# Gathering the experts' tokens unit by unit in fp32, with 17 instead of 14 weight slots, in a hybrid SSD, attention and expert layer

## The chip, the cores and the metric

The kernel runs on one core of a Trainium2 chip. The metric is the device time of one execution in microseconds, the median of several runs. One execution was also recorded by the hardware profiler; its rows are the ones shown below.

## What is computed

One layer for 512 tokens of width 1024: a norm, a wide projection, a state-space branch and a sliding-window attention branch, both gated and merged, an output projection added to x, a second norm, and 64 experts of which each token uses two. The part that the change touches, shortened:

```python
x = x + merged @ w_out
h2 = rms_norm(x, norm2_g).reshape(b * s, d)     # x * rsqrt(mean(x^2) + eps) * norm2_g
...
xs = h2[tok].reshape(n_blocks, MOE_BLOCK, -1)   # rows gathered by expert
def expert_block(args):
    xb, e = args
    hid = jax.nn.silu(xb @ w_gate_e[e]) * (xb @ w_up_e[e])
    return hid @ w_down_e[e]
...
return x + y_moe
```

## The kernel before, in words

The first 700 us (projections, both branches) are not touched. Then three stages follow.

The output projection (lines 711 to 773) runs over four column tiles `ct` of 256 columns. Its matmuls (L741 to L743) give the new x, which L746 adds to the old x in `acc`, four tiles of 128 tokens by 1024 columns. The same loop transposes x for the router (L751, L754, L758). It also multiplies x by norm2's weights along the row (L767, from `g2t`), and splits the product into a rounded high part (L772, ScalarE) and the rest (L773, GpSimd), both kept in `hx`, two tiles of 16 KB per partition. Each token's own norm factor is a scalar and is applied later, from `rst`, `rr` and `gts`.

The router (L796 to L845) chooses two experts for each token on VectorE and computes `dest`, a place for each of the 1024 assignments: expert e has places from 512 e on, and its first 32 are served by the main loop.

The main loop goes over `units`: 16 units of four experts and, after eight of them, unit 16, which serves 128 more tokens of one expert that has over 32. For each unit
- `group(g)`, called every second unit, gathers the tokens of two units: an indicator matrix `oh` (L879, L880 on VectorE) with 256 columns, and a matmul of `hx`, high and low, with `oh` into PSUM (L888), evicted to `st` (L893). The result is already transposed: 128 rows of the width by 256 slots;
- `products(u)` multiplies by the gate and up weights (L908, four experts side by side in the columns of the array; L903 in unit 16), applies tanh and two VectorE steps (L913 to L915), transposes (L918, L920), multiplies by the down weights (L929; L926 in unit 16) and splits the result for the way back (L934, L935);
- `combine` scatters the rows back with an indicator `wk` (L997, L998): two matmuls into PSUM (L1007, L1008) and an addition into `acc` (L1009) for each of 8 pieces.

The weights come from memory as 195 loads of 1024 KB, 12 for a unit (four experts times two gate/up halves and one down matrix) and 3 for unit 16. They go through a ring of slots: NA = 4 slots "ra", which lie where an early stage had its tiles and can be filled while the output projection still runs, and NB = 10 slots "rb", most of which lie where the output projection has its operands. `load_to` issues the next load (L783, on SyncE's queue) into a slot as soon as its last reader is done; SyncE works its queue in order.

The order of the instructions on each engine is set at build time by a list scheduler: an instruction that is ready in its own forecast of the run may be put ahead of earlier ones that are not. The buffers of a tag (such as the two PSUM buffers "tp", which `group` and `combine` share) go round in the order of the program. In memory the four tiles of `acc`, `hx` and the slots "ra" stand on one side; `oh`, `st`, `wk` and the slots "rb" on the other.

Of the kernel before, what the change touches and what calls it, by code (L numbers as in the profile page):

```python
# [7 lines left out]
F = mybir.dt.float32  # L8
R = mybir.dt.float32r
# [3 lines left out]
AF = mybir.ActivationFunctionType  # L13
# [8 lines left out]
CAP, BLK, NE, NBK, STEP = 32, 128, 64, 32, 512  # L22
POOL_LO, SSD_AHEAD, NA, NB, XGT, UX = 5, 1, 4, 10, 2, 8
PAD = 800
# [6 lines left out]
@with_exitstack  # L31
def tile_hybrid(ctx: ExitStack, tc: tile.TileContext, x, pos, cols, rows, g2d, wrd, wdtd, wcm, wqkv, wso, wao, wo,
                wgu, wdn, out):
    nc = tc.nc
# [50 lines left out]
    G.iota(av, pattern=[[1, 2], [256, 4]], base=1, channel_multiplier=2, allow_small_or_imprecise_dtypes=True)  # L85
    io4 = cp.tile([128, 256], F, name="io4")
    G.iota(io4, pattern=[[STEP, 8], [1, 32]], base=0, channel_multiplier=0, allow_small_or_imprecise_dtypes=True)
    io1 = cp.tile([128, 128], F, name="io1")
# [24 lines left out]
    bx = cp.tile([128, 1], F, name="bx")  # L113
    ixx = cp.tile([128, 3], I32, name="ixx")
    dram = ctx.enter_context(tc.tile_pool(name="dram", bufs=1, space=bass.MemoryType.DRAM))
    h2d = dram.tile([512, 1024], F, name="h2d")
# [583 lines left out]
    ring = [wslot(pr, "ra", NA) for i in range(NA)]  # L700
    hx = [pr.tile([128, 4, 1024], R, name=f"hx{i}") for i in range(2)]
    wrt = [v_(n=288), v_(n=288)]
    g2t = [v_(), v_()]
    for u in range(2):
        S.dma_start(wrt[u], wrd[:, u * 288:(u + 1) * 288])
        S.dma_start(g2t[u], _rows(g2d[u * 512:(u + 1) * 512], 512))
        for k in range(4):
            G.tensor_scalar(wrt[u][:, k * 72:(k + 1) * 72], wrt[u][:, k * 72:(k + 1) * 72],
                            n2g[:, 4 * u + k:4 * u + k + 1], None, op0=OP.mult)
    acc = [pr.tile([128, 1024], F, name=f"acc{t}") for t in range(4)]  # L710
    x2 = [[acc[t][:, u * 512:(u + 1) * 512] for u in range(2)] for t in range(4)]
    for t in range(4):
        nc.sync.dma_start(acc[t], x[t * 128:(t + 1) * 128])
    sx = v_(n=24)
# [9 lines left out]
    for ct in range(4):  # L724
# [4 lines left out]
        cu, cc = ct // 2, slice((ct % 2) * 256, (ct % 2 + 1) * 256)  # L729
        xg, xT = [c_(), c_()], [v_(), v_()]  # L730
        pt = [ptile("tp"), ptile("tp")]
# [30 lines left out]
        elif ct < 3:  # L762
            V.tensor_tensor(lg, lg, pl[:, 0:288], op=OP.add)
        for t in range(4):
            if ct == 3 and t == XGT:
                row_factors()
            (G if ct == 3 else V).tensor_tensor(xg[t // 2][:, (t % 2) * 256:(t % 2 + 1) * 256], x2[t][cu][:, cc],  # L767
                                                g2t[cu][:, cc], op=OP.mult)
        for tp in range(2):
            x3 = xg[tp].rearrange("p (t d) -> p t d", t=2)  # L770
            hi, lo = [hx[i][:, 2 * tp:2 * tp + 2, ct * 256:(ct + 1) * 256] for i in range(2)]
            S.activation(hi, x3, AF.Copy)  # L772
            G.tensor_tensor(lo, x3, hi.bitcast(F), op=OP.subtract)  # L773

# [96 lines left out]

    def group(g):
        dg = dest
        if g:
            dg = pm.tile([128, 8], F, name="dg", tag="dg", bufs=1)
            V.tensor_scalar(dg, dest, -8.0 * STEP * g, None, op0=OP.add)
        oh = pm.tile([128, 4, 256], R, name="oh", tag="oh", bufs=1)
        for t in range(4):
            V.tensor_scalar(oh[:, t], io4, dg[:, t:t + 1], None, op0=OP.is_equal)  # L879
            V.scalar_tensor_tensor(oh[:, t], io4, dg[:, 4 + t:5 + t], oh[:, t].bitcast(F), op0=OP.is_equal, op1=OP.add)  # L880
        st_ = pm.tile([128, 2048], F, name="st", tag="st", bufs=2)
        sts[g] = st_.rearrange("p (k c) -> p k c", k=8)
        for k in range(0, 8, 2):
            p = ptile("y" if g == 0 and k % 4 else "tp")
            for u in range(2):
                for h in range(2):
                    for t in range(4):
                        T.matmul(p[:, u * 256:(u + 1) * 256], hx[h][:, t, (k + u) * 128:(k + u + 1) * 128], oh[:, t],  # L888
                                 start=(h == 0 and t == 0), stop=(h == 1 and t == 3))
            if g == 0 and k % 4:  # L890
                V.tensor_copy(st_[:, k * 256:(k + 2) * 256], p)
            else:
                S.activation(st_[:, k * 256:(k + 2) * 256], p, AF.Copy)  # L893
            yield

    def products(u):
        pg = ptile("mm")
        ga = group(0) if u == 0 else None
        for k in range(8):
            if ga and k % 2 == 0:  # L900
                next(ga)
            if u == 16:
                T.matmul(pg, sts[16][:, k], wt[u, k // 4, 0][:, (k % 4) * 512:(k % 4 + 1) * 512],  # L903
                         start=(k == 0), stop=(k == 7))
                continue
            for e in range(4):
                c = u % 2 * 128 + e * 32
                T.matmul(pg[e * 32:(e + 1) * 32], sts[u // 2][:, k, c:c + 32],  # L908
                         wt[u, k // 4, e][:, (k % 4) * 512:(k % 4 + 1) * 512], start=(k == 0), stop=(k == 7))
# [139 lines left out]
    def over():  # L1049

        dg = pm.tile([128, 8], F, name="dg", tag="dg", bufs=1)
        V.tensor_scalar(dg, dest, bx, None, op0=OP.subtract)
        oh = pm.tile([128, 4, 128], R, name="oh", tag="oh", bufs=1, padded_shape=[128, 4, 256])
        ok = [m_().rearrange("p (t c) -> p t c", t=4) for k in range(2)]
        p = ptile("sb")
        for k in range(2):
            V.tensor_tensor(ok[k], io1[:, None, :].to_broadcast([128, 4, 128]),
                            dg[:, 4 * k:4 * k + 4, None].to_broadcast([128, 4, 128]), op=OP.is_equal)
            for t in range(4):
                T.matmul(p[:, 0:2], ok[k][:, t], rr[:, k, t], start=(k == 0 and t == 0), stop=(k == 1 and t == 3))  # L1060
        V.tensor_copy(rst[:, :, 16], p[:, 0:2])
        V.tensor_tensor(oh, ok[0], ok[1], op=OP.add)
        st_ = pm.tile([128, 1024], F, name="st", tag="st", bufs=2, padded_shape=[128, 2048])
        sts[16] = st_.rearrange("p (k c) -> p k c", k=8)
        for c in range(2):
            p = ptile("tp")
            for k in range(4):
                for h in range(2):
                    for t in range(4):
                        T.matmul(p[:, k * 128:(k + 1) * 128], hx[h][:, t, (4 * c + k) * 128:(4 * c + k + 1) * 128],  # L1070
                                 oh[:, t], start=(h == 0 and t == 0), stop=(h == 1 and t == 3))
            S.activation(st_[:, c * 512:(c + 1) * 512], p, AF.Copy)

    used = 0
    for u in units:
        load_to(used + NA + NB)
        used += 3 if u == 16 else 12
        wk = onehot(u) if u else None
        if u == 16:
            over()  # L1080
        yhl = products(u)
        if u == 0:
            places()
            wk = onehot(0)
        if u == 2:
            count()
        if u % 2 == 0 and u < 14:
            for _ in group(u // 2 + 1):
                pass
        combine(wk, yhl, u)  # L1090

    def extra(i):
# [69 lines left out]
        for t in range(4):  # L1162
            for u in range(2):
                hs = slice(u * 512, (u + 1) * 512)
                ht = m_()
                V.tensor_tensor(ht, hx[0][:, t, hs].bitcast(F), hx[1][:, t, hs].bitcast(F), op=OP.add)
                V.tensor_scalar(ht, ht, rr[:, 0, t, 0:1], 2.0, op0=OP.mult, op1=OP.mult)
                nc.sync.dma_start(h2d[t * 128:(t + 1) * 128, hs], ht)
# [14 lines left out]
        for tl, src, c, n in ((xg, h2d, 4, 512), (o, out, 4, 512), (gt, gwd, 3, 1024)):  # L1183
            V.memset(tl, 0.0)
            G.indirect_dma_start(out=tl, out_offset=None, in_=src, in_offset=at(c), bounds_check=n - 1,
                                 oob_is_err=False)
        xt = pm.tile([128, 1024], F, name="xt", tag="st", bufs=2, padded_shape=[128, 2048])
        for u in range(2):
            p = ptile("tp")
            for k in range(4):  # L1190
                s = slice(k * 128, (k + 1) * 128)
                T.transpose(p[:, s], xg[:, u * 512 + k * 128:u * 512 + (k + 1) * 128], ident)
            V.tensor_copy(xt[:, u * 512:(u + 1) * 512], p)
        p = ptile("mm")
# [27 lines left out]
def _layout(inp):  # L1222
# [14 lines left out]
    def tm(m):  # L1237
# [23 lines left out]
        ("rows", c(rows)),  # L1261
        ("g2", c(f["norm2_g"][0])),
        ("wr", c(wr.reshape(8, 128, 72).transpose(1, 0, 2).reshape(128, 576))),
# [27 lines left out]
```

## Time and profile before

| | before |
|---|---|
| time, median of 3 runs | 1267.71 us (1267.61 to 1268.23) |
| the profiled execution | 1267.16 us, span of its core 1265.4 us |
| TensorE matmul / weight load busy | 93% / 62% of the span |
| VectorE / ScalarE / GpSimd busy | 51% / 31% / 19% |
| read from memory | 266.47 MB, mean 216 GB/s over the span |

Busy shares are averages over stages with different limits: the first 700 us move few bytes, the expert stage moves most of them. The matmuls are recorded with ends that are modelled, so two records may overlap; the spacing of records in the chain is the better price of one.

### The profile page before, as it was taken

To read this page: it belongs to the slowest core of one execution; us is meant where nothing else is said; L and a number is where in the kernel's file an instruction comes from. 1 tells how busy PE (TensorE), PEld (TensorE's weight loads), DVE (VectorE), ACT (ScalarE), POOL (GpSimd) and SP (SyncE) were. 2 spreads that over 40 slices of the span, in tenths; PEclk is the share of its full clock that TensorE was granted. 3 is DMA by queue.
4 is the path that set the end of the run, shared out by engine and by line. 5 is a ranking of instruction groups with operands and counts; after the bars stand their busy time and mean duration, and the time that the engine had idled before them with its cause. 6 is when DMAs were issued, how large, how long until landed. Compare 5 with 4: busy or idle time off the path is not lost.

```text
span 1265.4 us, 16578 instructions
## 1 busy us (share of the span) xinstructions
PE 1177.4 (93%) x6552; PEld 789.3 (62%) x6552; DVE 651.2 (51%) x1224; ACT 388.6 (31%) x796; POOL 237.8 (19%) x189
## 2 busy tenths in 40 slices
PE   6999999999999999999999996989899799989885
PEld 5877878877888878887777994442424244424321
DVE  5956565568526667766647446443342234232422
ACT  5455453454326444534423330210111011101100
POOL 2033431143024522240020131010001000000000
PEclk9999999999999999999999997999999999999998
DMA  4321213211220222212145717999999999999995
GB/s 167 105 89 38 97 67 117 100 67 57 76 101 34 100 68 84 76 64 78 43 167 188 294 55 296 420 415 420 420 419 419 419 416 388 385 414 418 419 419 235
DMA packets 43120, 273.86 MB, mean 216 GB/s; under 512 B 5024, under 2 KB 5664, under 8 KB 11808
## 3 DMA queue, kind: packets, MB, share of 16 engines
q1 hardware_dynamic: 39744, 263.34, 52.7%
q0 software_dynamic: 1712, 7.34, 1.5%
q10 hardware_dynamic: 1584, 2.10, 0.6%
q8 instruction: 52, 0.85, 0.3%
q14 instruction: 28, 0.23, 0.1%
HBM read 266.47 MB, written 6.29 MB: 216 GB/s over the span
## 4 chain that ended last, share of the span: by engine, by line
PE 52%; DMA 6%; DVE 5%; ACT 1%; issue 1%; DVEq 0%; SPq 0%
PE mm L908 10%; PE y L929 6%; PE tp L888 5%; PE mm L197 4%; PE mm L198 4%; PE mm L199 4%; DMA rb<-in_wdn_dram 4%; PE tp L1007 3%; DVE acc L1009 2%; PE tp L1008 2%; PE sb L574 2%; DMA ra<-in_wdn_dram 2%; PE y L620 1%; PE sb L573 1%; PE mm L483 1%; PE mm L485 1%
## 5 line engine op out<-in xcount | busy, mean ns | idle before, releaser
L197 PE MATMUL mm<-h,g 128*128 128x512 f32 x448 | 180.7, 403 | 1.3 <-DVE c L309 1.0
L199 PE MATMUL mm<-h,g 128*128 128x512 f32 x448 | 178.3, 398 | 0.8 <-POOL g L183 0.7
L198 PE MATMUL mm<-h,g 128*128 128x512 f32 x448 | 178.2, 398 | 0.0
L908 PE MATMUL mm<-rb,st 128*32 128x512 f32 x712 | 144.7, 625 | 9.8 <-DMA rb<-in_wgu_dram 9.8
L182 ACT ACTIVATE g<-w 128x1024 fp32r<-128x1024 f32 x100 | 105.6, 1057 | 157.0 <-PE mm L198 113.1
L183 DVE TENSOR_TENSOR g<-w,g 128x1024 fp32r<-128x1024 f32 x78 | 96.8, 1240 | 70.4 <-ACT g L182 66.4
L1009 DVE TENSOR_TENSOR acc<-acc,tp 128x512 f32<-128x512 f32 x132 | 85.9, 684 | 34.4 <-PE tp L1008 34.3
L997 POOL TENSOR_SCALAR wk<-dr,vcol 128x512 fp32r<-128x512 int16 x17 | 26.6, 1565 | 385.4 <-PE tp L1008 347.9
L197 PEld LDWEIGHTS mm<-h,g 128*128 128x128 f32 x448 | 84.4, 188 | 22.7 <-issue 3.8
L199 PEld LDWEIGHTS mm<-h,g 128*128 128x128 f32 x448 | 84.2, 188 | 21.5 <-issue 2.3
L198 PEld LDWEIGHTS mm<-h,g 128*128 128x128 f32 x448 | 84.4, 188 | 18.8 <-issue 2.8
L183 POOL TENSOR_TENSOR g<-w,g 128x1024 fp32r<-128x1024 f32 x22 | 53.8, 2447 | 174.9 <-ACT g L182 143.6
L929 PE MATMUL y<-rb,n 128*32 128x512 f32 x384 | 77.0, 673 | 5.2 <-ACT n L920 3.3
L908 PEld LDWEIGHTS mm<-rb,st 128*32 128x32 f32 x712 | 31.3, 114 | 73.6 <-issue 55.0
L888 PEld LDWEIGHTS tp<-oh,hx 128*128 128x128 f32 x480 | 61.3, 194 | 22.3 <-issue 14.9
L935 DVE TENSOR_TENSOR yo<-y,yo 128x512 fp32r<-128x512 f32 x34 | 23.5, 691 | 99.0 <-ACT yo L934 99.0
L908 PE MATMUL mm<-ra,st 128*32 128x512 f32 x312 | 73.1, 596 | 0.0
L1007 PE MATMUL tp<-yo,wk 128*128 128x512 f32 x132 | 59.2, 465 | 12.7 <-DVE acc L1009 12.5
L888 PE MATMUL tp<-oh,hx 128*128 128x256 f32 x480 | 67.4, 293 | 3.6 <-DVE m L960 3.6
L1007 PEld LDWEIGHTS tp<-yo,wk 128*128 128x128 f32 x132 | 23.6, 187 | 68.9 <-DVE acc L1009 39.5
L913 ACT ACTIVATE n<-mm,rst 128x256 f32<-128x256 f32 x17 | 8.0, 473 | 177.0 <-PE mm L908 169.4
L484 PE MATMUL mm<-g,h 128*128 128x256 f32 x192 | 55.1, 287 | 0.9 <-DVE g L183 0.8
(375 smaller groups left out, 2257.5 us busy)
## 6 DMA issues: line engine op xcount, KB each, us to landing
rb<-in_wgu_dram SPq DMA_DIRECT2D x89, 1024.0 KB, 14.0
rb<-in_wdn_dram SPq DMA_DIRECT2D x48, 1024.0 KB, 16.9
ra<-in_wgu_dram SPq DMA_DIRECT2D x39, 1024.0 KB, 12.2
w<-in_wcm_dram SPq DMA_DIRECT2D x27, 1024.0 KB, 4.9
ra<-in_wdn_dram SPq DMA_DIRECT2D x16, 1024.0 KB, 16.6
w<-in_wso_dram SPq DMA_DIRECT2D x8, 1024.0 KB, 4.9
w<-in_wqkv_dram SPq DMA_DIRECT2D x6, 1024.0 KB, 4.9
gtd<-c POOLq DMA_DIRECT2D x16, 256.0 KB, 2.5
```

The lines of the kernel that those rows point to most:

```text
L182: S.activation(hi[:, :n], src, AF.Copy)
L183: (G if nsp[0] < 3 or nsp[0] % POOL_LO == 0 else V).tensor_tensor(lo[:, :n], src, hi[:, :n].bitcast(F), op=OP.subtract)
L197: T.matmul(p, hi[:, s], mh[k], start=(k == 0), stop=False)
L198: T.matmul(p, hi[:, s], ml[k], start=False, stop=False)
L199: T.matmul(p, lo[:, s], mh[k], start=False, stop=(k == 7))
L484: T.matmul(o, hh[k][:, ts], lo[:, s], start=False, stop=False)
L888: T.matmul(p[:, u * 256:(u + 1) * 256], hx[h][:, t, (k + u) * 128:(k + u + 1) * 128], oh[:, t], start=(h == 0 and t == 0), stop=(h == 1 an ...
L908: T.matmul(pg[e * 32:(e + 1) * 32], sts[u // 2][:, k, c:c + 32], wt[u, k // 4, e][:, (k % 4) * 512:(k % 4 + 1) * 512], start=(k == 0), sto ...
L929: T.matmul(py[n][e * 32:(e + 1) * 32], hT[:, f * 128 + e * 32:f * 128 + e * 32 + 32], wt[u, 2, e][:, ws], start=(f == 0), stop=(f == 1))
L997: G.tensor_scalar(wk, drow[0], vcol[:, b:b + 1], None, op0=OP.is_equal)
L1007: T.matmul(p, wk[:, t * 128:(t + 1) * 128], yhl[n][0], start=True, stop=False)
L1009: V.tensor_tensor(acc[t][:, ns], acc[t][:, ns], p, op=OP.add)
```

## The change

- `hx`, `xg`, `g2t` and the input `g2` go. The projection adds into new tiles `xc`; the gather reads `xc`, the whole fp32 sums.
- `acc` is a separate set of four tiles. GpSimd copies `xc` into it once, written behind unit 0's products.
- `gather(u)` and `fetch` take the place of `group(g)`: one unit at a time, an indicator of 128 columns in fp32, fp32 matmuls without high and low parts, and norm2's weights (now `n2c`, one per partition) applied by the eviction, 128 columns at a time, on ScalarE (in unit 0 half of them on VectorE).
- The gather of the next unit (or `over` for unit 16) is written between a unit's products and its combine.
- `oh` and `dg` have two buffers, `st` two of half the size. NA goes from 4 to 6 and NB from 10 to 11.
- `extra`, for experts with still more tokens, applies the weights behind its own transposes.

The diff, shortened:

```diff
-POOL_LO, SSD_AHEAD, NA, NB, XGT, UX = 5, 1, 4, 10, 2, 8
+POOL_LO, SSD_AHEAD, NA, NB, UX = 5, 1, 6, 11, 8
...
-    io4 = cp.tile([128, 256], F, name="io4")
-    G.iota(io4, pattern=[[STEP, 8], [1, 32]], base=0, channel_multiplier=0, allow_small_or_imprecise_dtypes=True)
+    io4 = cp.tile([128, 128], F, name="io4")
+    G.iota(io4, pattern=[[STEP, 4], [1, 32]], base=0, channel_multiplier=0, allow_small_or_imprecise_dtypes=True)
...
+    n2c = cp.tile([128, 8], F, name="n2c")
+    V.tensor_copy(n2c, n2g)
...
-    hx = [pr.tile([128, 4, 1024], R, name=f"hx{i}") for i in range(2)]
     wrt = [v_(n=288), v_(n=288)]
-    g2t = [v_(), v_()]
...
-        S.dma_start(g2t[u], _rows(g2d[u * 512:(u + 1) * 512], 512))
...
-    acc = [pr.tile([128, 1024], F, name=f"acc{t}") for t in range(4)]
-    x2 = [[acc[t][:, u * 512:(u + 1) * 512] for u in range(2)] for t in range(4)]
+    xc, acc = [[pr.tile([128, 1024], F, name=f"{n}{t}") for t in range(4)] for n in ("xc", "acc")]
+    x2 = [[xc[t][:, u * 512:(u + 1) * 512] for u in range(2)] for t in range(4)]
     for t in range(4):
-        nc.sync.dma_start(acc[t], x[t * 128:(t + 1) * 128])
+        nc.sync.dma_start(xc[t], x[t * 128:(t + 1) * 128])
...
-        for t in range(4):
-            if ct == 3 and t == XGT:
-                row_factors()
-            (G if ct == 3 else V).tensor_tensor(xg[t // 2][:, (t % 2) * 256:(t % 2 + 1) * 256], x2[t][cu][:, cc],
-                                                g2t[cu][:, cc], op=OP.mult)
-        for tp in range(2):
-            x3 = xg[tp].rearrange("p (t d) -> p t d", t=2)
-            hi, lo = [hx[i][:, 2 * tp:2 * tp + 2, ct * 256:(ct + 1) * 256] for i in range(2)]
-            S.activation(hi, x3, AF.Copy)
-            G.tensor_tensor(lo, x3, hi.bitcast(F), op=OP.subtract)
+        if ct == 3:
+            row_factors()
...
-    def group(g):
+    def gather(u):
         dg = dest
-        if g:
-            dg = pm.tile([128, 8], F, name="dg", tag="dg", bufs=1)
-            V.tensor_scalar(dg, dest, -8.0 * STEP * g, None, op0=OP.add)
-        oh = pm.tile([128, 4, 256], R, name="oh", tag="oh", bufs=1)
+        if u:
+            dg = pm.tile([128, 8], F, name="dg", tag="dg", bufs=2)
+            V.tensor_scalar(dg, dest, -4.0 * STEP * u, None, op0=OP.add)
+        oh = pm.tile([128, 4, 128], F, name="oh", tag="oh", bufs=2)
         for t in range(4):
             V.tensor_scalar(oh[:, t], io4, dg[:, t:t + 1], None, op0=OP.is_equal)
-            V.scalar_tensor_tensor(oh[:, t], io4, dg[:, 4 + t:5 + t], oh[:, t].bitcast(F), op0=OP.is_equal, op1=OP.add)
-        st_ = pm.tile([128, 2048], F, name="st", tag="st", bufs=2)
-        sts[g] = st_.rearrange("p (k c) -> p k c", k=8)
-        for k in range(0, 8, 2):
-            p = ptile("y" if g == 0 and k % 4 else "tp")
-            for u in range(2):
-                for h in range(2):
-                    for t in range(4):
-                        T.matmul(p[:, u * 256:(u + 1) * 256], hx[h][:, t, (k + u) * 128:(k + u + 1) * 128], oh[:, t],
-                                 start=(h == 0 and t == 0), stop=(h == 1 and t == 3))
-            if g == 0 and k % 4:
-                V.tensor_copy(st_[:, k * 256:(k + 2) * 256], p)
-            else:
-                S.activation(st_[:, k * 256:(k + 2) * 256], p, AF.Copy)
+            V.scalar_tensor_tensor(oh[:, t], io4, dg[:, 4 + t:5 + t], oh[:, t], op0=OP.is_equal, op1=OP.add)
+        return fetch(u, oh)
+
+    def fetch(u, oh):
+        st_ = pm.tile([128, 1024], F, name="st", tag="st", bufs=2)
+        sts[u] = st_.rearrange("p (k c) -> p k c", k=8)
+        n = 2 if u == 0 else 4
+        for c in range(0, 8, n):
+            p = ptile("y" if u == 0 and c % 4 else "tp")
+            for k in range(n):
+                for t in range(4):
+                    T.matmul(p[:, k * 128:(k + 1) * 128], xc[t][:, (c + k) * 128:(c + k + 1) * 128], oh[:, t],
+                             start=(t == 0), stop=(t == 3))
+            for k in range(n):
+                if k % 2 and u == 0:
+                    V.tensor_scalar(sts[u][:, c + k], p[:, k * 128:(k + 1) * 128], n2c[:, c + k:c + k + 1], None,
+                                    op0=OP.mult)
+                else:
+                    S.activation(sts[u][:, c + k], p[:, k * 128:(k + 1) * 128], AF.Copy, scale=n2c[:, c + k:c + k + 1])
             yield
...
         wk = onehot(u) if u else None
-        if u == 16:
-            over()
         yhl = products(u)
         if u == 0:
             places()
             wk = onehot(0)
+            for t in range(4):
+                G.tensor_copy(acc[t], xc[t])
         if u == 2:
             count()
-        if u % 2 == 0 and u < 14:
-            for _ in group(u // 2 + 1):
-                pass
+        i = units.index(u) + 1
+        if i < len(units):
+            if units[i] == 16:
+                over()
+            else:
+                for _ in gather(units[i]):
+                    pass
         combine(wk, yhl, u)
```

`over` fills its own indicator as before and then calls `fetch(16, oh)` in place of its own copy of the gather.

## Rows read from the trace of the kernel before

**Rows 1.** The page: GB/s in 40 equal slices; weight loads with size.

```profile
GB/s 167 105 89 38 97 67 117 100 67 57 76 101 34 100 68 84 76 64 78 43 167 188 294 55 296 420 415 420 420 419 419 419 416 388 385 414 418 419 419 235
...
rb<-in_wgu_dram SPq DMA_DIRECT2D x89, 1024.0 KB, 14.0
```

**Rows 2.** Stretches: length, busy us of each engine (instructions), clock, DMA share, GB/s.

```profile
720.00:752.00 32.00, 31.30 (x265) 31.09 (x264) 15.46 (x31) 10.54 (x25) 7.61 (x6) 1.00 0.03 13
778.00:787.00 9.00, 9.00 (x78) 4.74 (x77) 1.55 (x4) 1.20 (x2) 0.00 (x0) 1.00 0.09 14
787.00:1044.00 257.00, 232.21 (x1347) 102.55 (x1344) 92.64 (x194) 31.04 (x58) 18.98 (x14) 0.97 1.01 418
1044.00:1107.00 63.00, 59.76 (x342) 28.77 (x345) 22.60 (x42) 8.14 (x15) 4.69 (x3) 0.97 0.95 387
...
928.00:950.00 22.00, 19.28 (x112) 6.24 (x104) 8.09 (x14) 2.05 (x4) 1.50 (x1) 0.92 1.01 419
1179.00:1200.00 21.00, 18.09 (x116) 6.06 (x114) 7.88 (x14) 2.05 (x4) 1.56 (x1) 1.00 1.01 418
```

**Rows 3.** The timeline of SyncE's DMA issues: start, us, queue, line, destination and source, count.

```profile
714.70 41.12 SPq L783 DMA_DIRECT2D rb<-in_wgu_dram  x4
...
785.45 1.96 SPq L783 DMA_DIRECT2D ra<-in_wgu_dram  x4
```

**Rows 4.** Who TensorE waited for after 780 us: total us, times, longest.

```profile
PE sb L918 <- DVE n L915: 19.1, 12, 1.9
...
PE mm L908 <- DMA rb<-in_wgu_dram: 9.8, 6, 3.7
PE y L929 <- ACT n L920: 5.2, 11, 0.5
```

**Rows 5.** The chain that ended last, in order of time: start, us, engine, line, records.

```profile
781.06 1.85 PE mm L908 x16
...
810.90 1.85 PE mm L908 x16
...
870.63 7.00 PE mm L908 x58
...
894.30 3.98 PE tp L888 x32
...
927.85 7.00 PE mm L908 x58
...
937.28 5.36 PE y L929 x32
...
950.29 2.02 PE tp L888 x16
...
1012.91 7.37 PE tp L1070 x64
...
1024.75 3.63 PE mm L903 x8
...
1179.32 7.04 PE mm L908 x60
...
1188.79 3.68 PE y L929 x32
```

**Rows 6.** TensorE's timeline: after unit 13's combine, and unit 15's last y.

```profile
1200.32 0.62 PE L908 MATMUL mm<-rb,st 128*32 128x512 f32 x2
...
1248.07 3.62 PE L929 MATMUL y<-rb,n 128*32 128x512 f32 x20 [0.26 <-DMA rb<-in_wdn_dram]
```

**Rows 7.** GpSimd's and VectorE's timelines in the router.

```profile
760.27 2.59 POOL L773 TENSOR_TENSOR hx<-c,hx 128x512 fp32r<-128x512 f32 x2
...
760.63 1.07 DVE L811 TENSOR_TENSOR v<-v 128x32 f32<-128x32 f32 x1
...
764.82 0.19 DVE L811 TENSOR_TENSOR v<-v 128x32 f32<-128x32 f32 x1
```

More of the change, by code (lines that the diff above doesn't have):

```diff
@@ L31, in tile_hybrid @@
 @with_exitstack
-def tile_hybrid(ctx: ExitStack, tc: tile.TileContext, x, pos, cols, rows, g2d, wrd, wdtd, wcm, wqkv, wso, wao, wo,
+def tile_hybrid(ctx: ExitStack, tc: tile.TileContext, x, pos, cols, rows, wrd, wdtd, wcm, wqkv, wso, wao, wo,
                 wgu, wdn, out):
@@ L729, in tile_hybrid @@
         cu, cc = ct // 2, slice((ct % 2) * 256, (ct % 2 + 1) * 256)
-        xg, xT = [c_(), c_()], [v_(), v_()]
+        xT = [v_(), v_()]
         pt = [ptile("tp"), ptile("tp")]
@@ L897, in products @@
         pg = ptile("mm")
-        ga = group(0) if u == 0 else None
+        ga = gather(0) if u == 0 else None
         for k in range(8):
@@ L906, in products @@
             for e in range(4):
-                c = u % 2 * 128 + e * 32
-                T.matmul(pg[e * 32:(e + 1) * 32], sts[u // 2][:, k, c:c + 32],
+                T.matmul(pg[e * 32:(e + 1) * 32], sts[u][:, k, e * 32:(e + 1) * 32],
                          wt[u, k // 4, e][:, (k % 4) * 512:(k % 4 + 1) * 512], start=(k == 0), stop=(k == 7))
@@ L1049, in over @@
     def over():
-        dg = pm.tile([128, 8], F, name="dg", tag="dg", bufs=1)
+        dg = pm.tile([128, 8], F, name="dg", tag="dg", bufs=2)
         V.tensor_scalar(dg, dest, bx, None, op0=OP.subtract)
-        oh = pm.tile([128, 4, 128], R, name="oh", tag="oh", bufs=1, padded_shape=[128, 4, 256])
+        oh = pm.tile([128, 4, 128], F, name="oh", tag="oh", bufs=2)
         ok = [m_().rearrange("p (t c) -> p t c", t=4) for k in range(2)]
@@ L1062, in over @@
         V.tensor_tensor(oh, ok[0], ok[1], op=OP.add)
[L1063 to L1072, printed above, removed]
+        for _ in fetch(16, oh):
+            pass
     used = 0
@@ L1084, in tile_hybrid @@
             wk = onehot(0)
+            for t in range(4):
+                G.tensor_copy(acc[t], xc[t])
         if u == 2:
             count()
-        if u % 2 == 0 and u < 14:
-            for _ in group(u // 2 + 1):
-                pass
+        i = units.index(u) + 1
[4 more added lines that the diff above has]
+                for _ in gather(units[i]):
+                    pass
         combine(wk, yhl, u)
@@ L1165, in extra @@
                 ht = m_()
-                V.tensor_tensor(ht, hx[0][:, t, hs].bitcast(F), hx[1][:, t, hs].bitcast(F), op=OP.add)
-                V.tensor_scalar(ht, ht, rr[:, 0, t, 0:1], 2.0, op0=OP.mult, op1=OP.mult)
+                V.tensor_scalar(ht, xc[t][:, hs], rr[:, 0, t, 0:1], 2.0, op0=OP.mult, op1=OP.mult)
                 nc.sync.dma_start(h2d[t * 128:(t + 1) * 128, hs], ht)
@@ L1186, in extra @@
                                  oob_is_err=False)
-        xt = pm.tile([128, 1024], F, name="xt", tag="st", bufs=2, padded_shape=[128, 2048])
+        xt = pm.tile([128, 1024], F, name="xt", tag="st", bufs=2)
         for u in range(2):
@@ L1192, in extra @@
                 T.transpose(p[:, s], xg[:, u * 512 + k * 128:u * 512 + (k + 1) * 128], ident)
-            V.tensor_copy(xt[:, u * 512:(u + 1) * 512], p)
+            for k in range(4):
+                V.tensor_scalar(xt[:, (4 * u + k) * 128:(4 * u + k + 1) * 128], p[:, k * 128:(k + 1) * 128],
+                                n2c[:, 4 * u + k:4 * u + k + 1], None, op0=OP.mult)
         p = ptile("mm")
@@ L1261, in _layout @@
         ("rows", c(rows)),
-        ("g2", c(f["norm2_g"][0])),
         ("wr", c(wr.reshape(8, 128, 72).transpose(1, 0, 2).reshape(128, 576))),
```

## The prediction

> **What bounds the kernel now.** I read the page's slices first, then a table of stretches, then SyncE's issue list, and only then TensorE's waits and the chain. From the middle of the span the transfers run flat at 419 to 420 GB/s [rows 1]: the 64 experts' weights come as loads of 1024 KB, so one load takes 1.0486 MB / 419.5 GB/s = 2.50 us, a unit of four experts (12 loads) 30.0 us. The reader should see that the stream is the first limit and that it loses time in three places [rows 2]. Between 720 and 752 us it carries 13 GB/s: only the four "ra" slots are loaded ahead of it, and the first "rb" load is held until the output projection's last matmul lets its space go; the four issues that begin at 714.70 take 41.12 us [rows 3]. Between 778 and 787 it carries 14 GB/s: all 14 slots are full and the first is handed back at 785.45. Between 1044 and 1107 it runs at 387 instead of 419.5, a loss of 63 x 0.077 = 4.9 us, because TensorE hands slots back late there.
>
> TensorE is hardly slower than the stream. After 780 us it waits only 9.8 us for gate/up weights in front of the expert products (L908), against 19.1 us for the two DVE steps ahead of the transposes (L918) and 5.2 us for ACT ahead of y (L929) [rows 4]. So there are two near limits, and a change that moves the one is soon held by the other. The chain gives a unit's length on TensorE [rows 5]: from L908 to the next unit's work, unit 3 takes 894.30 - 870.63 = 23.7 us, unit 5 22.4, unit 13 (to 1200.32 [rows 6]) 21.0; mean 22.4. Those have no gather in them. With a gather unit 4 takes 927.85 - 894.30 = 33.6.
>
> **What the change costs TensorE.** Before, one group serves two units: 8 column blocks x (high, low) x 4 token tiles = 64 matmuls of 256 columns. After, each unit has its own: 8 x 4 = 32 matmuls of 128 columns in full fp32. An fp32 matmul is two records in the trace (the eight of L903 appear as 16), so it is 64 records again, now per unit. Price of one: the old ones run at 3.98 / 32 = 0.124 us. From below, 64 records of 128 columns in the reduced form took 7.37 us, 0.115 each. From above, L903's 512-column fp32 records take 3.63 / 8 = 0.454, which is 0.027 over 1024 cycles at 2.4 GHz; 256 cycles plus the same 0.027 is 0.134 [rows 5]. I take 0.125, nearest to the records with as many column passes: 8.0 us a unit (7.4 to 8.6). The gathers of units 0 and 16 have as many records as before; the eight groups become 16 gathers, so 8 x 8.0 = 64 us of TensorE work are added. (The Trainium skill, FP8 and Floating Point Precision, TensorE Precision Notes, gives true fp32 four passes. The trace agrees: 2 x 0.454 us is 4.26 times 512 columns at 2.4 GHz. By four passes alone a gather would be an estimated 6.8 us and the sum below some 17 us shorter.)
>
> **What hides it.** The new gather of the next unit stands between a unit's products and its combine and its target buffer is free once the unit before has been multiplied. It can therefore run where TensorE now idles: 1.5 us ahead of the transposes and 0.47 ahead of y, which is 24.3 us over 23 waits [rows 4]. Before, a group was ready for that place only every second unit and stood after a combine instead [rows 5]. Filling the gap takes 2.0 us off a unit. It may also keep the clock up: y takes 3.68 us in unit 13 and 5.36 in unit 5, whose stretches were granted 1.00 and 0.92 of full speed [rows 2]; I count 0.8 of these 1.7 us. A unit with its gather becomes 22.4 + 8.0 - 2.0 - 0.8 = 27.6; I take 27.2, since a lone L908 matmul between other work should be rarer when gather records stand ready in its place. Bounds of that unit: 26.6 (gather 7.4) and 30.4 (nothing filled).
>
> **TensorE's sum.** Start of the first products 781.1, less 1 for the shorter router (below): 780. Unit 0 keeps 29.8 (it had a whole group before too). Units 1 to 14: 14 x 27.2 = 381. Counting the experts' tokens in unit 2: an estimated 4, the same before and after. Unit 16: 28, a unit of one expert with a gather. Unit 15 to the end: 7.0 for products, 2.5 for the gaps, 3.7 for y and 1265.4 - 1251.7 = 13.7 from y's end [rows 6], 27. Together 1250. The same sum for the kernel before (781 + 29.8, 14 x 22.4, six groups at 8.0 with an estimated 1.9 for lone matmuls around each, where unit 4 shows 33.6 - 22.4 - 8.0 = 3.2, counting 4, unit 16 at 22.4 + 7.4, the end 27, and the 9.8 of waits for weights) gives 1254.5 against 1265.4. It misses 11 us; I carry 8 of them over, since some hang on waits for weights that a deeper queue shortens: 1258.
>
> **The stream's sum.** Slots go from 14 to 17. Two more "ra" slots are loaded behind the first four, into the empty stretch; one more "rb" slot is loaded in the empty stretch before 787 [rows 2, 3]. Three loads less remain when the first slot comes back: 3 x 2.50 = 7.5 us. The deeper queue can also win back up to 6 us of the dips, or none if TensorE stays late. The end is then 1265.4 - 7.5 - (0 to 6) = 1252 to 1258, the tail after the last landing (1248.07 [rows 6]) unchanged. Both sums meet at 1258.
>
> **The small parts.** The weighted copies, their split and the g2 rows vanish from the output projection: DVE and POOL get lighter there, but TensorE was busy 31.30 of 32 us [rows 2], so at most 0.7 us. In the router, L811 took 1.07 us instead of 0.19 while POOL subtracted [rows 7]; without that, 1 to 2 us. Against it stand POOL's four new copies into acc; no wait orders them behind the router, and their operands are ready when the projection ends. Price: nothing if they come later, else up to four times the 2.59 us that POOL needed for as many elements in two pieces [rows 7]. Net I take 1 us gained, between 2 gained and 8 lost. The indicator tiles are eight half-width DVE operations for each unit where eight full ones served two; DVE was busy 93 of 257 us at 0.48 us a piece [rows 2], and two buffers let it run ahead: nothing, or 8 x 0.25 = 2 us a unit if it stood on the path. Applying norm2's weights turns four evictions for two units into eight per unit; at ACT's mean 0.53 us that is 4 us of a unit, and ACT was busy 31 of 257 us: nothing, or one last eviction of 0.5 us ahead of the combine, which lies within the bounds above. On SyncE's queue the two extra loads can stand ahead of the projection's last weight loads; they are 5 us of transfer in a stretch that carries 13 GB/s [rows 2], so nothing. The x rows go to xc by the same four loads as to acc before.
>
> **The rivals.** (1) The gather doesn't fill the gaps. The instruction order is fixed at build time; if it puts the gather ahead of the products, as the groups stand now, TensorE sets the pace: 30.4 a unit, 14 x 3.2 = 45 us more than my sum when it happens in all units, 22 in half of them: span 1280 to 1303, time 1282 to 1305, slower. For it: all six groups after unit 0 stand so. Against: in unit 0, where a group was ready, it did fill the gap. It decides from 27.7 us a unit on. (2) The gaps fill well, records cost 0.115 and the deeper queue removes the dips: only the stream is left, span 1248 to 1252, time 1250 to 1254. For it: 419 GB/s wherever slots are free. (3) POOL's copies run in the router and hold it for 4 to 8 us: every later load shifts with the first slot handed back, 1264 to 1268 in time, no change. For it: the rows of L773 and L811 [rows 7]. Against: the copies can start while the projection still runs. (The Trainium skill, SBUF — State Buffer, SBUF: two separate sides, says that a DVE operation with two SBUF inputs is shut out for the whole length of a GpSimd operation that reads SBUF. The rows agree: L811 ends only when the first half of L773 has ended.)
>
> **How the numbers follow.** The median of the runs is 2.3 us above the profiled span (the profiled execution's own time 1.8): 1258 + 2 = 1260. Chances: forecast 0.50 (1252 to 1272, of which 0.07 fall into no change and 0.05 beyond), rival 1 0.30, rival 2 0.12, rival 3 0.08 (0.06 no change). What a measurement can tell from no change is about 0.2%, 2.5 us. Faster: 0.38 + 0.12 + 0.02 = 0.52; same 0.13; slower 0.35. The range, 1248 to 1292, leaves out the worse half of rival 1 and little below.
>
> **What would show it.** Right: 17 loads issued before the first slot returns; transfers of 419 GB/s from there on; units of 27 to 28 us with gather records between L908 and the transposes, and hardly any wait in front of the transposes. Wrong: waits ahead of the transposes as long as before, the stream falling below 400 GB/s over many units, SyncE waiting for products: then TensorE sets the pace and the extra slots bring nothing. A first product later than 782 us would show rival 3.

## The result: 1314 us, slower by 3.7%

| | before | after |
|---|---|---|
| time, median | 1267.66 us | 1314.07 us (1312.74 to 1315.2) |
| ratio | | 1.037, 95% interval 1.0357 to 1.0383 |
| the profiled execution | 1267.16 us, span 1265.4 | 1314.59 us, span 1312.8 |

The forecast was 1260 us in a range of 1248 to 1292: the sign was wrong and the time lies outside the range. Lines of after that the text uses: products L903 (L899 in unit 16), gather matmul L882, its eviction L889, transposes L913, y L924, scatter L1002 and L1003, addition L1004, weight loads L774.

The page of after, GB/s in the 40 slices. Against [rows 1] the flat 419 ends at the 29th slice; from there TensorE returns slots too slowly.

```profile
GB/s 169 99 80 65 73 89 83 94 65 65 96 97 33 97 65 94 36 97 56 106 145 327 83 244 419 420 420 420 419 416 404 331 331 320 361 406 384 386 372 67
```

After in stretches (columns as in [rows 2]). The stretch from 1044 loses bandwidth although TensorE is busy 61.61 of 63 us.

```profile
787.00:1044.00 257.00, 241.78 (x1511) 121.16 (x1508) 90.64 (x213) 36.59 (x100) 18.95 (x14) 0.97 1.00 412
1044.00:1107.00 63.00, 61.61 (x378) 32.67 (x377) 21.38 (x51) 10.42 (x32) 3.12 (x2) 1.00 0.75 299
1140.00:1230.00 90.00, 82.87 (x476) 38.09 (x477) 28.39 (x55) 10.68 (x29) 4.68 (x3) 0.96 0.98 397
```

Who TensorE waited for after 780 us. Not one wait for a weight is left (9.8 us for gate/up weights in [rows 4]), and the wait ahead of the transposes, which the gather was to fill, is what it was: 19.0 against 19.1 us.

```profile
PE sb L913 <- DVE n L910: 19.0, 12, 1.7
PE tp L1002 <- DVE acc L1004: 7.3, 20, 0.6
PE y L924 <- ACT n L915: 6.2, 12, 0.9
```

One unit in the chain that ended last, in order of time (start, us, engine, line, records). This is where most of the 47 us of span are lost.

```profile
1173.82 5.36 PE y L924 x32
...
1179.84 0.98 PE mm L903 x2
...
1181.48 0.97 PE mm L903 x2
...
1183.57 0.98 PE mm L903 x2
...
1187.32 3.55 PE mm L903 x26
1190.87 1.98 PE tp L882 x16
1192.86 0.97 PE mm L903 x2
1193.83 2.43 PE tp L882 x20
1196.26 0.97 PE mm L903 x2
1197.23 3.10 PE tp L882 x26
1200.33 0.97 PE mm L903 x2
1201.31 0.42 PE tp L882 x2
1201.73 3.56 PE mm L903 x26
...
1207.73 5.36 PE y L924 x32
```

From y to y it is 33.9 us: y 5.36, the combine with three products in it 8.1 (to 1187.32), 26 product records 3.55, the gather 1.98 + 2.43 + 3.10 + 0.42 = 7.9, three more products inside the gather 2.9, the last 26 records 3.56, and 2.4 to the next y, in which TensorE has only the two transposes. The gather stands ahead of the end of the products instead of behind it, so it hides nothing. Six of the 32 product matmuls stand alone (in most other units five): 0.97 us each. Four that use the array's columns together need about 0.86 us (26 records, that is three groups of four and one alone, take 3.55). The Trainium skill, TensorEngine Tiling (Array Packing), Tiling Modes, says that different tiles of the array can work in parallel; the 0.97 for one and 0.86 for four agree.

### The profile page after: what moved, and what is told of

Same layout as the page of the kernel before. It is cut to its first block, busy times and chain, and to the rows that moved or that the text cites. A ratio compares the mean times of both kernels' runs of the same rounds, so it can differ in the third digit from the quotient of the medians.

```text
span 1312.8 us, 17737 instructions
## 1 busy us (share of the span) xinstructions
PE 1244.4 (95%) x7064; PEld 849.3 (65%) x7064; DVE 656.4 (50%) x1287; ACT 402.3 (31%) x888; POOL 227.7 (17%) x181
## 3 DMA queue, kind: packets, MB, share of 16 engines
q0 software_dynamic: 1712, 7.34, 1.5%
## 4 chain that ended last, share of the span: by engine, by line
PE 59%; DVE 4%; ACT 1%; DMA 1%; issue 1%; POOL 0%; DVEq 0%; SPq 0%; POOLq 0%
PE mm L903 13%; PE tp L882 10%; PE y L924 6%; PE mm L199 4%; PE mm L200 4%; PE mm L201 4%; PE tp L1002 3%; PE tp L1003 2%; DVE acc L1004 2%; PE sb L576 2%; PE y L622 1%; PE sb L575 1%; PE mm L485 1%; PE mm L487 1%; PE mm L486 1%; PE mm L740 1%
## 5 line engine op out<-in xcount | busy, mean ns | idle before, releaser
L882 PEld LDWEIGHTS tp<-oh,xc 128*128 128x128 f32 x1056 | 124.3, 193 | 41.8 <-issue 37.0
L882 PE MATMUL tp<-oh,xc 128*128 128x128 f32 x1056 | 134.2, 281 | 4.0 <-DVE rr L951 3.1
L903 PE MATMUL mm<-rb,st 128*32 128x512 f32 x624 | 132.2, 597 | 0.0
L889 ACT ACTIVATE st<-tp,n2c 128x128 f32<-128x128 f32 x130 | 37.2, 368 | 252.8 <-PE tp L882 252.8
L1004 DVE TENSOR_TENSOR acc<-acc,tp 128x512 f32<-128x512 f32 x132 | 85.9, 684 | 54.9 <-PE tp L1003 54.7
L903 PE MATMUL mm<-ra,st 128*32 128x512 f32 x400 | 88.3, 597 | 0.0
L870 DVE TENSOR_SCALAR oh<-io,dg 128x128 f32<-128x128 f32 x60 | 13.8, 300 | 107.8 <-PE tp L882 101.6
L1002 PE MATMUL tp<-yo,wk 128*128 128x512 f32 x132 | 59.2, 463 | 8.0 <-DVE acc L1004 7.8
L924 PE MATMUL y<-rb,n 128*32 128x512 f32 x336 | 62.7, 724 | 3.8 <-ACT n L915 3.8
L1002 PEld LDWEIGHTS tp<-yo,wk 128*128 128x128 f32 x132 | 23.7, 187 | 63.6 <-DVE acc L1004 33.4
L903 PEld LDWEIGHTS mm<-rb,st 128*32 128x32 f32 x624 | 27.1, 109 | 48.5 <-issue 44.1
## 6 DMA issues: line engine op xcount, KB each, us to landing
rb<-in_wgu_dram SPq DMA_DIRECT2D x78, 1024.0 KB, 12.9
```

Source lines behind the costliest of these rows:

```text
L882: T.matmul(p[:, k * 128:(k + 1) * 128], xc[t][:, (c + k) * 128:(c + k + 1) * 128], oh[:, t], start=(t == 0), stop=(t == 3))
L889: S.activation(sts[u][:, c + k], p[:, k * 128:(k + 1) * 128], AF.Copy, scale=n2c[:, c + k:c + k + 1])
L903: T.matmul(pg[e * 32:(e + 1) * 32], sts[u][:, k, e * 32:(e + 1) * 32], wt[u, k // 4, e][:, (k % 4) * 512:(k % 4 + 1) * 512], start=(k == 0 ...
L924: T.matmul(py[n][e * 32:(e + 1) * 32], hT[:, f * 128 + e * 32:f * 128 + e * 32 + 32], wt[u, 2, e][:, ws], start=(f == 0), stop=(f == 1))
L1002: T.matmul(p, wk[:, t * 128:(t + 1) * 128], yhl[n][0], start=True, stop=False)
L1004: V.tensor_tensor(acc[t][:, ns], acc[t][:, ns], p, op=OP.add)
```

## Experiments

**The gather behind the products.** The next unit's gather, and `over`, are ordered behind the unit's last product matmul on TensorE; no wait is added and nothing else is changed.

```diff
-                T.matmul(pg[e * 32:(e + 1) * 32], sts[u][:, k, e * 32:(e + 1) * 32],
+                last[0] = T.matmul(pg[e * 32:(e + 1) * 32], sts[u][:, k, e * 32:(e + 1) * 32],
...
-            if units[i] == 16:
-                over()
...
+            with tc.issue_after(last[0].ins):
+                if units[i] == 16:
+                    over()
...
```

> The changed kernel, with one edge more for each unit: the matmuls of the next unit's gather are issued behind the unit's last gate/up product, on TensorE alone and without a wait. Nothing is left out. Theory 1 (the place costs it): in the changed kernel the gather stands in front of and between the products, so 2.4 us ahead of the transposes and y stay empty, y runs partly at the lower clock, and about three more products run alone. A unit falls from 33 us to 26, TensorE gets ahead of the stream, and the end is the first slot's return at 790 + 178 loads x 2.50 + 1.5 + a tail of 17 = 1254 us of span, 1256 of time. Theory 2 (the work costs it): 64 records more in each second unit take their time wherever they stand; the time stays at 1300 to 1314.

Measured: 1263.51 us, ratio to before 0.996 (0.995 to 0.997). 50.6 us come back by order alone; the 7.5 us above theory 1's 1256 are taken up under "Both" and "The bias row" below. TensorE's waits after 780 us in this kernel: the transposes wait once, and the waits for weights are there again, as the stream is now the limit.

```profile
PE mm L904 <- DMA ra<-in_wgu_dram: 8.8, 7, 1.7
...
PE mm L904 <- DMA rb<-in_wgu_dram: 2.5, 4, 1.1
PE sb L914 <- DVE n L911: 1.5, 1, 1.5
```

The filled gap is only one part of the 50.6 us. The waits ahead of the transposes and y fall from 25.2 to 2.0 us. The busy time of the products alone and of y alone after 780 us (the figure behind the stretch's length; the first pair of rows is the products, the second y, each in after and then in this kernel) falls by 17 and 14 us, as fewer products stand alone and y no longer runs at the lower clock. Against that, some 12 us of waits for weights are new.

```profile
780.00:1313.00 533.00, 182.14 (x1024) 37.65 (x1024) 0.97 0.90 368
780.00:1313.00 533.00, 164.98 (x1024) 37.51 (x1024) 0.98 0.89 368
...
780.00:1313.00 533.00, 79.76 (x512) 22.23 (x512) 0.97 0.90 368
780.00:1313.00 533.00, 65.57 (x512) 17.62 (x512) 0.98 0.89 368
```

**The lone products.** After's own gather, but each unit's products ordered behind the last scatter matmul of the unit before; that takes three of the six lone products out of the combine.

```diff
-        for k in range(8):
...
+        with tc.issue_after(done[0].ins) if u else ExitStack():
+            for k in range(8):
...
-                T.matmul(p, wk[:, t * 128:(t + 1) * 128], yhl[n][1], start=False, stop=True)
+                done[0] = T.matmul(p, wk[:, t * 128:(t + 1) * 128], yhl[n][1], start=False, stop=True)
```

> The changed kernel with each unit's products issued behind the last scatter matmul of the unit before, and no other edit (the gather stays where it is). That takes three of the six products per unit that stand alone among scatter or gather matmuls out of the scatter, and puts them together. In the changed kernel a product that stands alone takes 0.97 us, and four that share the array 0.86 us together. Theory (what the unit costs above the forecast is partly its lone products, each about 0.75 us more than in a group): 3 x 0.75 = 2.2 us less per unit, some 30 us less in 14 units: 1279 to 1290. Rival (a product alone costs no more than its share, the gather's place is all): 1308 to 1316.

Measured: 1288.38 us, ratio 1.0165 (1.0141 to 1.0188): 25.7 us less than after, near the 30 of the first theory, but not by that theory alone. The products' own busy time falls by the 30 (182.14 to 152.23 us). y falls as well, by 16 (79.76 to 63.85), since it runs at the higher clock in most units here. Against both, the bare combine now waits for its additions, 20.3 us against 7.3 in after: a product among the scatter matmuls wasn't all loss. That the net comes near 30 is partly luck. The busy time of the products and of y, and the waits, all after 780 us:

```profile
780.00:1313.00 533.00, 152.23 (x1024) 34.46 (x1024) 0.98 0.89 366
...
780.00:1313.00 533.00, 63.85 (x512) 18.77 (x512) 0.98 0.89 366
...
PE tp L1004 <- DVE acc L1006: 20.3, 46, 1.0
PE sb L915 <- DVE n L912: 17.4, 11, 1.7
```

**Half a gather.** The gather of every unit but the first sums only over the first 256 of the 512 tokens, so part of the experts' rows stays empty.

```diff
-                for t in range(4):
+                for t in range(4 if u == 0 else 2):
...
```

> The changed kernel with half of the gather's matmuls left out for every unit but the first (the gather then sums over the first 256 tokens only, so that part of the experts' rows stays empty); order and placement are the scheduler's own. Theory (while TensorE sets the end and nothing hides the gather, its records cost their own time): 32 records of 0.115 us less in each of 15 units, 3.7 x 15 = 55 us, cut short where the weight stream takes over, near 1263: 1258 to 1270. Rival (the gather's matmuls stand in time in which the products would wait for their weights anyway): 1300 to 1316.

Measured: 1263.31 us (ratio 0.9967, 0.9955 to 0.9979), 50.8 us less than after. The same 1263 as with the whole gather in the right place: two ways of making TensorE shorter than the stream end at the same stream (420 GB/s between 1044 and 1107 us in both, 299 in after).

**Fewer slots in after.** NA and NB as before the change: 4 and 10.

```diff
-POOL_LO, SSD_AHEAD, NA, NB, UX = 5, 1, 6, 11, 8
+POOL_LO, SSD_AHEAD, NA, NB, UX = 5, 1, 4, 10, 8
```

> The changed kernel with the old 4 + 10 weight slots instead of 6 + 11; nothing else differs. Theories 1 and 2: TensorE sets the pace and never waits for weights, so the three slots bring nothing: 1311 to 1317. If the slots were worth what the stream's sum gave them (three loads at the start), 7.5 us more: 1321 or later.

Measured: 1311.93 us (1.0338, 1.0312 to 1.0364). While TensorE paces, the three slots are worth nothing.

**The addresses.** In after the last weight load of the projection is issued at 722.13 us, in before at 714.33, though no instruction of the first 700 us was touched. The constants are 480 bytes per partition shorter (`io4` 512 less, `n2c` 32 more), so that all tiles allocated behind them on that side lie 480 bytes lower. A tile that nobody uses restores this.

```diff
     V.tensor_copy(n2c, n2g)
+    cp.tile([128, 120], F, name="shift")
```

> The changed kernel with an unused tile of 480 bytes behind the constants, so that the tiles on that side of the memory lie at the addresses that they had in the kernel before (there the indicator's row of numbers was 512 bytes longer and n2c's 32 bytes were missing). Nothing is left out. Theory 3 (addresses): the first 700 us are 7 us longer in the changed kernel since the projections' matmuls that stream from h step at 0.233 us instead of 0.229; with the old addresses 4 to 7 us come back: 1307 to 1310. Rival: it is the chip or the run, and the time stays at 1312 to 1315.

Measured: 1303.42 us (1.0288, 1.0252 to 1.0324), 10.7 less than after, where 4 to 7 were expected; the last projection load is issued at 715.94. Two of the three lines that stream `h`, between 50 and 700 us (name, shape, count, busy us, mean ns); first after, then with the unused tile:

```profile
L199 PE MATMUL mm<-h,g 128*128 128x512 f32 x410 | 166.3, 406 | 0.9 <-DVE c L311 0.9
L200 PE MATMUL mm<-h,g 128*128 128x512 f32 x411 | 164.7, 401 | 0.0
```

```profile
L200 PE MATMUL mm<-h,g 128*128 128x512 f32 x412 | 166.0, 403 | 0.9 <-DVE c L312 0.9
L201 PE MATMUL mm<-h,g 128*128 128x512 f32 x412 | 164.0, 398 | 0.0
```

3 ns on each of some 1340 matmuls is 4 us, and 6.2 were won by 716 us: part of that is a stretch from 500 to 600 us that was granted 0.98 in after and 1.00 here. The recorded execution is the fastest of the four (1299.08 us; its span of 1297.3 is 15.5 under after's), and most of what it won later lies in y: 71.34 us after 780 us against 79.76, with the instructions in the same order. So the address change is not shown to be worth all of the 10.7.

```profile
780.00:1313.00 533.00, 71.34 (x512) 20.39 (x512) 0.98 0.89 363
```

**Which addresses.** The gather behind the products, and 32 unused bytes, so that the tiles lie 448 bytes lower, a multiple of 64.

```diff
     V.tensor_copy(n2c, n2g)
+    cp.tile([128, 8], F, name="shift")
```

> The gather placed behind each unit's last product, and 32 unused bytes in place of 480, so that the left-side tiles stand 448 bytes lower than in the kernel before (a multiple of 64) instead of 480 lower (a multiple of 32 only). If it is the remainder of the address that slows the matmuls which stream h: means of the three lines 403, 398, 397 ns again and 1257 to 1260 us. If it is where exactly the tiles stand: 405, 401, 401 ns as without it, and 1262 to 1265 us.

Measured: 1262.47 us (0.9963, 0.9951 to 0.9975), with means of 405, 401 and 401 ns:

```profile
L200 PE MATMUL mm<-h,g 128*128 128x512 f32 x410 | 166.0, 405 | 0.9 <-DVE c L312 0.9
L201 PE MATMUL mm<-h,g 128*128 128x512 f32 x410 | 164.3, 401 | 0.0
```

So it isn't the remainder by 64 that counts. What about the place of the tiles does it stays open.

**Both.** The gather behind the products and the 480 unused bytes.

> Both edits at once. Theories 1 and 3 together: the stream's end 1256 less 5 to 7, so 1249 to 1251, below the kernel before. Theory 2 with theory 3: 1294 to 1308.

Measured: 1258.44 us (0.992, 0.9896 to 0.9944): faster than both kernels, but 7 us above the expectation. The stream runs at 419 to the end, so it started late. In after's issue list on SyncE (start, us, queue, line, destination and source, count) the rb loads begin at 767.08, where before they began at 714.70 + 41.12 = 755.82 [rows 3]:

```profile
722.13 0.33 SPq L726 DMA_DIRECT2D w<-in_wo_dram  x1
767.08 0.80 SPq L774 DMA_DIRECT2D rb<-in_wgu_dram  x2
...
790.17 2.00 SPq L774 DMA_DIRECT2D ra<-in_wgu_dram  x3
```

VectorE's timeline says what they waited for: L790 reads the router's bias row (`rowt`) until 767.06.

```profile
766.53 0.53 DVE L790 TENSOR_TENSOR v<-rowt,v 128x32 f32<-128x32 f32 x2
```

With eleven rb slots one of them reaches over `rowt`, and it is the first to be loaded. Its load waits for the router's first step, and the ten behind it, whose space is free when the projection's last matmul ends, wait in SyncE's queue with it.

**The bias row out of the way.** Both edits as in the last experiment, and the bias row is copied early into a tile of its own (288 bytes; with 192 unused ones that is 480 again).

```diff
+    brc = cp.tile([128, 72], F, name="brc")
+    V.tensor_copy(brc, brt)
+    cp.tile([128, 48], F, name="shift")
...
-        V.tensor_tensor(b3[:, :, c], brt[:, None, c].to_broadcast([128, 4, c.stop - c.start]),
+        V.tensor_tensor(b3[:, :, c], brc[:, None, c].to_broadcast([128, 4, c.stop - c.start]),
```

> The gather placed behind each unit's last product, the router's bias row copied early into a tile of its own (288 bytes), and 192 unused bytes, so that the left side stands at before's addresses again. Compared with the kernel that has the placement and the addresses alone (1258.4 us). Theory (the first of the eleven rb loads waited for the router's bias step L792 and held up the ten behind it): that wait of SyncE is gone, ten loads are issued about 758.6, when the projections end, instead of 763, one of them a little earlier, and the stream and the end move by 4 to 6 us: 1252 to 1255. Rival (TensorE's own sum, or the return of the first slot at 785, sets the end): loads start earlier, the last product doesn't: 1257 to 1259.

Measured: 1251.36 us (0.9875, 0.9856 to 0.9894), 7 us less than without the copy, a little below the expected 1252 to 1255, and 16 less than before. SyncE's issues in it: rb loads from 714.28 + 38.29 = 752.57 on, and the first slot returned at 781.08.

```profile
714.28 38.29 SPq L777 DMA_DIRECT2D rb<-in_wgu_dram  x2
753.18 2.26 SPq L777 DMA_DIRECT2D rb<-in_wdn_dram  x4
...
781.08 1.28 SPq L777 DMA_DIRECT2D ra<-in_wgu_dram  x3
```

The two recorded executions are 9.2 us of span apart (1258.7 and 1249.5), and 4.0 of these lie ahead of the last projection load (717.91 without the copy, 713.91 here; the former was granted 0.98 from 400 to 600 us, the latter 1.00). Behind that load the copy is worth 540.8 - 535.6 = 5.2 us to the end, within the theory's 4 to 6. One unit in its chain, with the gather in its place (start, us, engine, line, records):

```profile
1100.50 3.59 PE y L928 x32
...
1111.88 6.98 PE mm L907 x58
1118.86 3.77 PE tp L886 x32
...
1122.85 3.57 PE tp L886 x32
1126.42 3.59 PE y L928 x32
```

25.9 us from y to y: half the gather on either side of the transposes, no gap, and y 3.59 instead of 5.36 us.

**The slots, where the stream is the limit.** The last kernel with 4 and 10 slots.

> The same kernel with 4 and 10 slots, as before the change. Theory (the prediction's term: while the stream sets the end, each slot that is loaded in the empty stretch ahead of the first products is worth one load of 2.50 us): 5 us longer for the two ra slots, 7.5 us for all three, so 1258 to 1262. Rival (slots are worth nothing here either): the same as with 17 slots within 1 us.

Measured: 1264.26 us (0.9978, 0.9968 to 0.9989), 12.9 more, above the expected 1258 to 1262. The stretches of both, first with 14 slots, then with 17, show what comes on top of the three loads: the dip between 1000 and 1100 us, 401 against 417 GB/s, is 100 x 16 / 419.5 = 4 us.

```profile
1000.00:1100.00 100.00, 98.58 (x621) 52.59 (x621) 40.27 (x89) 15.80 (x44) 6.26 (x4) 1.00 0.98 401
```

```profile
1000.00:1100.00 100.00, 97.87 (x613) 54.10 (x612) 39.87 (x87) 15.95 (x46) 6.25 (x4) 1.00 1.01 417
```

7.5 + 4 = 11.5; the first slot comes back 1.4 us later (782.50 against 781.08), which is about the rest.

**The kernel before with its own gather placed.** `group` is ordered behind the unit's last product, nothing else.

> The kernel before the change with its own gather (split copies, two units at once) placed behind the unit's last product, nothing else. If TensorE's waits ahead of the transposes (19 us in all) set its end, filling them brings 10 us or more: 1250 to 1258. If the weight stream sets its end, as its 1265.4 us of span by loads say, filling them brings nothing: 1266 to 1269; the waits on n would go down and waits for weights come up by about as much.

Measured: 1265.41 us (0.9981, 0.9969 to 0.9992). Before was held by its stream: the order brings 2 us, and while the waits ahead of the transposes fall from 19.1 to 12.4 us, those for gate/up weights rise from 9.8 to 17.7. With 14 slots, the order and the addresses equal, the new gather gives 1264.26 (with the copy of the bias row) and the old one 1265.41; their intervals overlap. So a gain of the new form by itself is not shown, and where the stream is the limit it could hardly show; what is shown is the worth of the three slots that it makes room for, 12.9 us.

## Why the prediction was wrong, step by step

- **"What hides it" failed, and decided the sign.** The step said that the new gather *can* run in the gap ahead of the transposes and counted it there for the likeliest case. The order on TensorE is fixed at build time, and it put the gather ahead of and among the products. The waits ahead of the transposes stayed at 19.0 us, against 19.1. The one edit that moves the gather gives 50.6 us. The gap of 2.0 us was as read; filling it was a matter of order, not of readiness. I weighed the evidence wrongly: all six groups after unit 0 stood ahead of the products, and one exception, in unit 0, stood against them. That one is `group(1)`, written behind unit 0's products just as the new gather is (64 records in before's chain from 792.85 us on, around the transposes of L918):

```profile
792.85 0.90 PE tp L888 x6
...
797.30 1.26 PE tp L888 x9
798.56 0.22 PE sb L918 x2
...
799.64 2.00 PE tp L888 x17
...
807.11 3.79 PE tp L888 x32
```

In after the gather of the next unit again stands in the gap of unit 0 (34 records from 798.05, then the transposes at 802.05), but as many waits ahead of the transposes remain as before, 12. So a place behind the products in the program didn't settle the place on TensorE; what makes unit 0 differ was not tried.

- **The lone products were missed, with the wrong sign.** The unit was taken as 27.2 instead of 27.6 "since a lone L908 matmul ... should be rarer". They stand alone five or six times in most units, at 0.97 us. Taking three away made the products 30 us shorter and the kernel 25.7.
- **The clock term was too small, and hung on more than the gap.** It counted 0.8 of 1.7 us for y. In after y takes 5.3 to 5.4 us in eight of the eleven units 3 to 7 and 9 to 14; in the best kernel, placed and in one piece, 3.59. With the unused tile alone, where the gap is as empty (18.9 us of waits), it is 5.4 in only two of these eleven units, and a unit is 31.6 on average from unit 9's y to unit 14's. A filled unit is 25.9, better than the 27.2 forecast, and an unfilled one about 33 (y to y 33.1 on average for units 2 to 7, 32.6 for 9 to 14), worse than rival 1's 30.4; some 1 us of that excess is the clock. From 32.9 to 27.2 it is 5.7 us in ten intervals, 57 us; 3 more from unit 7's y to unit 9's, around unit 16 (85.5 us against 28 + 2 x 27.2); the first product at 785.96 instead of 780, 6; less the 8 us carried over: 58, against 54.8 between the forecast and the measured span. The 3 us too many I did not trace.
- **The gather's price was nearly right.** 3.77 + 3.57 = 7.34 us for 64 records in the best kernel, 0.115 each, at the lower bound; I had taken 0.125. The estimate by the four passes of the Trainium skill (FP8 and Floating Point Precision, TensorE Precision Notes), 6.8 us, was about as far off below as my 8.0 above.
- **The stream's sum was right in size, but not for this kernel.** Three loads and 0 to 6 us of dips, 7.5 to 13.5: measured 12.9 in the best kernel. In after the slots do nothing (1311.93 with 14), as the text said for a slow TensorE.
- **SyncE's queue failed.** The step looked at the two added ra loads ("so nothing", which held) and not at what the added rb slot lies over. That slot stands first in the queue and holds ten others from the projection's end to the router's first step; 5 us once the stream is the limit, hidden in after.
- **A cost that no step named.** The early stages became slower by 7.8 us at the last projection load, through addresses and some stretches at a lower clock. The sum took the time up to 780 us as untouched.
- **The small parts held.** From the last projection load to the first slot returned, before took 785.45 - 714.33 = 71.1 us, after 790.17 - 722.13 = 68.0: 3 us won, and rival 3 did not come. But its sign ("a first product later than 782") did appear, for another reason: such a sign has to be measured from an event close by.
- **The rivals.** Rival 1 came, with the right mechanism but too small a price (1282 to 1305 against 1314), as it had neither the lone products nor the late first product in it, and with too small a chance. Rival 2, 1250 to 1254, is what the kernel gives once the order, the addresses and the bias row are mended: 1251.36.

## What to carry to other kernels

Before work is counted as hidden in a gap, look at where the builder of the instruction order has put the same work in the kernel at hand, and price the case in which it stays there; a cheap order that adds no wait can be worth more than the change. If a slot is added to a ring, look at which old tile it lies over, when that tile's last reader runs, and what stands behind that load in its queue. When constants change in size, compare the untouched stages first.

## What was unexpected of the hardware

- Moving tiles by 448 or 480 bytes per partition slowed matmuls that stream 512 columns of `h` from 403, 398, 398 to 405 or 406, 401, 401 ns. Lines of the same loop that stream `y` kept 400, 396, 395 ns.
- One 32-column product alone costs 0.97 us, four in different column tiles 0.86 us together.
- The same y takes 5.36 us in most units of after, and 3.59 right behind gather matmuls. From 1173.82 to 1179.18 us, one such y of after, TensorE was granted 0.68 of full speed, so part of the time the lower of its two levels, 1.2 GHz; in the best kernel 1100 to 1200 us were granted 1.00, 2.4 GHz throughout. The wait ahead of y isn't the whole cause. With the unused tile alone, the order and the waits are those of after (18.9 us ahead of the transposes), yet y took 3.6 to 3.7 us in nine of the eleven units counted above; with the products behind the combine, 17.4 us of such waits, it took 3.7 to 3.8 in most units. What else decides was not tried.
